# A hybrid diffusion backbone on one core: another queue for modulation weights, another order of the convolution's second product, and X formed half by half

## The chip, the cores and the metric

The kernel runs on one core of a Trainium2 chip. The time is the device time of the program in microseconds. Before the change three runs took 1233.27, 1236.50 and 1236.87 us, median 1236.5 us.

## The reference

Two layers run over 256 latent tokens of width 1024; 256 context tokens take part in layer 0. Each layer is a half-step FFN, a mixer and a half-step FFN, and each of these is

```python
h_lat = sublayer(h_lat, m_lat, 0, ffn1, FFN_HALF)
def sublayer(h, m, i, fn, res_w):
    y = fn(modulate(h, m[3 * i], m[3 * i + 1]))            # h * (1 + scale) + shift
    return layer_norm(ALPHA * h + res_w * m[3 * i + 2] * y, ln_g[l, i], ln_b[l, i])
def swiglu(h, w_in, w_out):
    gate, up = jnp.split(h @ w_in, 2, axis=-1)
    return (jax.nn.silu(gate) * up) @ w_out
```

The nine modulation vectors of a layer are `silu(c) @ w_ada[l] + b_ada[l]`, a product of one row with a 1024 x 9216 matrix. The mixer of layer 0 is differential attention with pooling. The mixer of layer 1 is a convolution module:

```python
a, g = jnp.split(h @ w_c1 + b_c1, 2, axis=-1)
z = a * jax.nn.sigmoid(g)
z = depthwise_conv(z, w_dw, 31 taps) + b_dw
z = jax.nn.silu(layer_norm(z, ln_g, ln_b))
return z @ w_c2 + b_c2
```

All inputs are float32.

## The kernel before

**Numbers.** A float32 product is made of three products of a reduced float32 format: each operand is split into a high part (a cast on ScalarE) and a low part (the difference, on VectorE), and `mm3` (L209) multiplies high by high, low by high and high by low. Activations are held as `XH` and `XL`, transposed: 128 channels on the partitions, eight channel blocks, tokens along the row.

**Weights.** All weights come as a list of jobs (`w_add`, L117), mostly 1 MB, in the order of use. `pump_load` (L120) issues a job's load on SP's queue into one of three `raw` buffers. Each job is cut into pieces of 1024 columns, here called weight tiles. `pump_split` (L143) makes the high part `wh` on ScalarE (L150) and the low part `wl` on VectorE (L151), or on GpSimd for a few of the convolution's; it takes buffers from the pool `wp` (six of each), or from another pool when the dictionary `alt` names one for that tile at the moment of the split. `wnext` (L154) hands out the next weight tile and splits up to five ahead.

**Order.** The program is traced in Python; a scheduler then orders the instructions of each engine by priority (the order of tracing, raised by `high_priority`) as they become ready in its own model of time. On the chip every engine works strictly in that order, and so does every queue of loads. `issue_after(i)` puts what is traced inside it behind instruction `i` on the same engine, without any other wait; `behind_x` (L277) does so behind the last forming of X.

**Modulation.** `ada_jobs` (L226) makes, for one modulation vector, eight pairs of a load (512 KB of weights, L236, on SP's queue) and a product with a sum on VectorE (L240), and a `fin` step on GpSimd (L248 to L257), which for a gate also writes the vector to DRAM and reads it back as a row over all partitions. The list `bg` holds them; `bgstep` (L289) is called once per weight tile in the FFNs and pops entries at an even rate (24, 32 and 8 products over 44 steps in the three lean FFNs), and `bg_one` (L265) issues the loads of the next entries before it pops one. In the lean FFNs (`sub_ffn`, L917) two load buffers rotate. They are the second FFN of layer 0, the first and the second of layer 1.

**The lean FFNs.** 44 weight tiles of the gate and up products, then 22 of the output product. The first two pairs of columns are done token tile by token tile: first 36 matmuls with token tile 0, then 36 with token tile 1, so that X of token tile 1 may be formed behind the first ones (`to_x_behind`). After them `flush` (L497) issues the affine part of the last layer norm of h on GpSimd (`affine`, L368): for each of two token tiles it loads the row `ln_g` on GpSimd's queue, multiplies two halves, loads `ln_b`, and adds two halves.

**X.** `to_x` (L321) transposes a normalized token tile on TensorE in two halves of four 128 x 128 blocks, scales and shifts each block (L333 on VectorE, L335 on ScalarE, in turn) and splits each half (L217): the high part on ScalarE, the low part on VectorE for the first half and on GpSimd for the second.

**The convolution module.** The first product takes 16 weight tiles. Four of the eight channel groups are convolved on TensorE with banded weights (L1137): for each group two runs (g) of 16 products into one PSUM tile, and after each run ScalarE takes it out (L1138). One group is done by ScalarE and GpSimd, three by VectorE, tap by tap (L998). `back` (L1041) transposes the finished groups, VectorE takes statistics, both engines normalize (`yn`), and TensorE transposes again before the SiLU (L1164) and the split. Six of the eight weight tiles of the second product are split ahead of the whole TensorE convolution (L1113). The second product (L1170 to L1184) computes the first 512 columns for both token tiles, then the other 512; `evac` (L383) adds the result to h, and `ln_norm` and `to_x` follow for each token tile.

## Time and profile before

| | |
|---|---|
| median of three runs | 1236.5 us |
| profiled execution | 1233.74 us |
| its span, first to last instruction | 1231.9 us |
| TensorE matmuls busy | 1181.1 us (96%) |
| VectorE busy | 882.7 us (72%) |
| ScalarE busy | 503.2 us (41%) |
| GpSimd busy | 206.7 us (17%) |
| mean granted clock of TensorE | 0.987 |
| loads from HBM | 269.38 MB, 220 GB/s over the span |

PE is TensorE, DVE is VectorE, ACT is ScalarE, POOL is GpSimd, SP is SyncE, which only issues loads. In a row of the timeline a bracket gives the idle time of that engine just before the row and what ended it; x is the number of instructions merged into the row. A matmul in full flow shows about 0.39 us, but they overlap: the distance of two starts is shorter. A granted clock of 1.00 is 2.4 GHz. In time, the second FFN of layer 0 lies at about 525 to 715 us, the first FFN of layer 1 at 715 to 921, the convolution module at 913 to 1037, and the last FFN behind it.

### The profile page before, as it was taken

What the parts mean: (1) busy time and instruction counts of PE and PEld (TensorE: products, weight loads), DVE (VectorE), ACT (ScalarE), POOL (GpSimd) and SP (SyncE); (2) the same over time, 40 slices, a digit from 0 to 9 for tenths busy, and PEclk for the clock granted to TensorE, in tenths of its full rate; (3) what the DMA queues carried; (4) which work ended last, traced back from release to release, by engine and by line L of the source; (5) the groups of instructions that cost most, each with busy time, mean ns of one, the idle gap of its engine ahead of it and who ended that gap; (6) DMA issues with size and microseconds to landing.
All of it is one profiled execution on the core that took longest, in us unless ns stands there. A gap on an engine that the chain in (4) does not pass through costs nothing.

```text
span 1231.9 us, 14930 instructions
## 1 busy us (share of the span) xinstructions
PE 1181.1 (96%) x5632; PEld 979.7 (80%) x5632; DVE 882.7 (72%) x1287; ACT 503.2 (41%) x731; POOL 206.7 (17%) x207
## 2 busy tenths in 40 slices
PE   6999999999999999999999999997999888999997
PEld 5888888888887887778888878886879877888885
DVE  5799987773337858798785688877667957875554
ACT  4243123222233546564444444433448333544431
POOL 0001020031003122134010033000017911330000
PEclk9899999999999999999999999998999989999999
DMA  9778688862232432369885748987648445975550
GB/s 361 306 252 290 230 275 308 271 223 100 86 124 65 161 137 103 137 233 336 329 299 186 265 167 337 326 315 274 220 164 297 145 178 168 322 279 184 175 188 35
DMA packets 59656, 272.60 MB, mean 221 GB/s; under 512 B 6592, under 2 KB 8256, under 8 KB 44224
## 3 DMA queue, kind: packets, MB, share of 16 engines
q1 hardware_dynamic: 56048, 259.56, 59.2%
q0 software_dynamic: 3536, 12.09, 3.0%
q8 instruction: 44, 0.72, 0.2%
q14 instruction: 28, 0.23, 0.1%
HBM read 269.38 MB, written 1.08 MB: 220 GB/s over the span
## 4 chain that ended last, share of the span: by engine, by line
PE 48%; DVE 7%; DMA 6%; ACT 2%; issue 2%; POOL 1%; DVEq 0%; SPq 0%; ACTq 0%; POOLq 0%
PE lf L212 7%; PE lf L210 6%; PE lf L211 6%; DMA ada<-in_wada 6%; PE of L210 4%; PE of L212 4%; PE of L211 4%; PE pc L1137 2%; DVE wl L151 2%; DVE ada L240 1%; PE c L210 1%; PE c L211 1%; PE c L212 1%; PE ltrf L435 1%; PE v L210 1%
## 5 line engine op out<-in xcount | busy, mean ns | idle before, releaser
L150 ACT CAST wh<-raw 128x1024 fp32r<-128x1024 f32 x309 | 321.6, 1051 | 466.6 <-PE of L212 128.3
L151 DVE TENSOR_TENSOR wl<-raw,wh 128x1024 fp32r<-128x1024 f32 x302 | 379.2, 1271 | 150.3 <-ACT wh L150 149.3
L210 PE MATMUL lf<-wh,XH 128*128 128x512 f32 x528 | 208.5, 395 | 3.8 <-ACT XH L217 3.6
L240 DVE SCALAR_TENSOR_TENSOR ada<-ada,crow 128x1024 f32<-128x1024 f32 x128 | 163.1, 1282 | 68.3 <-DMA ada<-in_wada 67.6
L212 PE MATMUL lf<-wh,XL 128*128 128x512 f32 x528 | 207.0, 392 | 0.4 <-DVE XL L217 0.4
L211 PE MATMUL lf<-wl,XH 128*128 128x512 f32 x528 | 206.0, 390 | 0.0
L210 PE MATMUL of<-wh,GHf 128*128 128x512 f32 x344 | 135.1, 393 | 0.0
L212 PE MATMUL of<-wh,GLf 128*128 128x512 f32 x344 | 134.5, 391 | 0.0
L211 PE MATMUL of<-wl,GHf 128*128 128x512 f32 x344 | 134.5, 391 | 0.0
L210 PEld LDWEIGHTS lf<-wh,XH 128*128 128x128 f32 x528 | 99.2, 188 | 25.0 <-ACT XH L217 5.5
L212 PEld LDWEIGHTS lf<-wh,XL 128*128 128x128 f32 x528 | 99.1, 188 | 23.2 <-DVE XL L217 2.3
L211 PEld LDWEIGHTS lf<-wl,XH 128*128 128x128 f32 x528 | 99.2, 188 | 20.0
L211 PEld LDWEIGHTS of<-wl,GHf 128*128 128x128 f32 x344 | 65.0, 189 | 13.4
L212 PEld LDWEIGHTS of<-wh,GLf 128*128 128x128 f32 x344 | 64.9, 189 | 13.6
L210 PEld LDWEIGHTS of<-wh,GHf 128*128 128x128 f32 x344 | 65.0, 189 | 13.3
L248 POOL TENSOR_TENSOR m<-m,cols 128x8 f32<-128x8 f32 x19 | 13.9, 731 | 358.0 <-DVE ada L240 213.3
L210 PE MATMUL gf<-XH,wh 128*128 128x512 f32 x152 | 59.1, 389 | 0.0
L211 PE MATMUL gf<-XL,wh 128*128 128x512 f32 x152 | 59.1, 389 | 0.0
L212 PE MATMUL gf<-XH,wl 128*128 128x512 f32 x152 | 59.1, 389 | 0.0
L210 PE MATMUL uf<-XH,wh 128*128 128x512 f32 x152 | 59.1, 389 | 0.0
L211 PE MATMUL uf<-XL,wh 128*128 128x512 f32 x152 | 59.1, 389 | 0.0
L212 PE MATMUL uf<-XH,wl 128*128 128x512 f32 x152 | 59.1, 389 | 0.0
(296 smaller groups left out, 1948.2 us busy)
## 6 DMA issues: line engine op xcount, KB each, us to landing
raw<-in_wfl SPq DMA_DIRECT2D x66, 1024.0 KB, 6.8
ada<-in_wada SPq DMA_DIRECT2D x128, 512.0 KB, 5.4
raw<-in_wfo SPq DMA_DIRECT2D x40, 1024.0 KB, 5.0
raw<-in_wfi SPq DMA_DIRECT2D x22, 1024.0 KB, 6.2
raw<-in_wc SPq DMA_DIRECT2D x10, 1024.0 KB, 6.6
wcv<-in_wcv SPq DMA_DIRECT2D x16, 512.0 KB, 4.7
aw<-in_wsh SPq DMA_DIRECT2D x8, 512.0 KB, 10.4
aw<-in_wsc SPq DMA_DIRECT2D x8, 512.0 KB, 9.9
```

The lines of the kernel that those rows point to most:

```text
L150: act.copy(wh[:, :w], r[:, off:off + w])
L151: lo_ins[q] = (pool if q in pool_lo else dve).tensor_tensor(wl[:, :w], r[:, off:off + w], wh[:, :w].bitcast(F32), ALU.subtract)
L210: pe.matmul(ps, lh, rh, start=first, stop=False)
L211: pe.matmul(ps, lh, rl, start=False, stop=False)
L212: last_mm[0] = pe.matmul(ps, ll, rh, start=False, stop=last)
L240: dve.scalar_tensor_tensor(st["raw"] if s == streams[-1] else crow["junk"], st["raw"], 1.0, crow[s], ALU.mult, ALU.mult, accum_out=mcol[l, ...
L248: pool.tensor_tensor(m, m, col("bad", (l * 9 + v) * 8, 8), ALU.add)
L435: pe.transpose(tr[:, j * W + t * P:j * W + (t + 1) * P], sg[:, t, j * P:(j + 1) * P], ident)
L1137: last = pe.matmul(pc[:, g * P:(g + 1) * P], wt[:, tap % 8 * P:(tap % 8 + 1) * P], z2, start=tap == 0, stop=tap == 15)
```

## The change

The second product's weights are loaded by depth quarter, both column halves in one load. The modulation loads of the lean FFNs go to GpSimd's queue; the first two of them are issued after X of token tile 1, ahead of the affine steps; each product on VectorE is placed behind the newest weight split. In `to_x` the scalings of the second half are placed behind the first half's, and on ScalarE behind the first half's cast. Six splits that were traced ahead of the TensorE convolution are traced two by two behind the evacuations of its first three runs. The second product does all of token tile 0, then all of token tile 1; the splits of the following weight tiles and the evacuations are placed by hand.

```diff
--- before.py
+++ after.py
@@ -195,9 +195,8 @@
         w_add(a["wcl"][:, hh * 2048:(hh + 1) * 2048], (1024, 1024))
     for j in range(2, 8):
         w_add(a["wc1"][j].rearrange("u p f -> p u f"), (1024, 1024))
-    for n in range(2):
-        for kk in range(2):
-            w_add(a["wc2"][n, :, kk * 2048:(kk + 1) * 2048], (1024, 1024))
+    for q in range(4):
+        w_add(a["wc2"][:, :, q * 1024:(q + 1) * 1024].rearrange("n p f -> p n f"), (1024, 1024))
     add_ffn(1, 1, 2, PARTS2)
     for ji, (_, widths) in enumerate(jobs):
         off = 0
@@ -222,6 +221,7 @@
     bg = []
     cur_ada = [None]
     NADS = [3]
+    ada_queue = [nc.sync]
 
     def ada_jobs(l, v, streams, gate=None, then=None):
 
@@ -233,7 +233,7 @@
 
             def load(j=j, st=st):
                 st["raw"] = cur_ada[0].tile([P, D], F32, tag="adaraw", name=f"ada{l}{v}{j}", bufs=NADS[0])
-                nc.sync.dma_start(st["raw"], a["wada"][l, v, j])
+                ada_queue[0].dma_start(st["raw"], a["wada"][l, v, j])
 
             def unit(j=j, st=st):
                 for s in streams:
@@ -262,12 +262,18 @@
 
     rate = [0.0, 0.0]
 
-    def bg_one():
+    def bg_load():
         for pre, _, _ in bg[:NADS[0]]:
             if pre is not None and id(pre) not in done:
                 done[id(pre)] = pre
                 pre()
-        with behind_x():
+
+    def bg_one():
+        bg_load()
+        with behind_x(), ExitStack() as st:
+            if ada_queue[0] is pool:
+
+                st.enter_context(tc.issue_after(lo_ins[len(ready) - 1].ins))
             bg.pop(0)[1]()
 
 
@@ -322,6 +328,7 @@
 
         xm = xmp[0].tile([P, KT, P], F32, tag="xm", bufs=xmp[1], name="xm" + name)
         ins = []
+        xd = xa = None
         for half in range(2):
             tr = trt(f"tr{name}{half}")
             for j in range(4):
@@ -329,12 +336,17 @@
                 pe.transpose(tr[:, j * P:(j + 1) * P], src_of[:, k * P:(k + 1) * P], ident)
             for j in range(4):
                 k = half * 4 + j
-                if func == AF.Identity and j % 2 == 0:
-                    dve.tensor_scalar(xm[:, k, :], tr[:, j * P:(j + 1) * P], A[:, k:k + 1], B[:, k:k + 1], ALU.mult, ALU.add)
-                else:
-                    act.activation(xm[:, k, :], tr[:, j * P:(j + 1) * P], func, bias=B[:, k:k + 1], scale=A[:, k:k + 1])
+                with ExitStack() as after:
+                    for i in (xd, xa):
+                        if i is not None:
+                            after.enter_context(tc.issue_after(i.ins))
+                    if func == AF.Identity and j % 2 == 0:
+                        xd = dve.tensor_scalar(xm[:, k, :], tr[:, j * P:(j + 1) * P], A[:, k:k + 1], B[:, k:k + 1], ALU.mult, ALU.add)
+                    else:
+                        xa = act.activation(xm[:, k, :], tr[:, j * P:(j + 1) * P], func, bias=B[:, k:k + 1], scale=A[:, k:k + 1])
             sl = slice(half * 4, half * 4 + 4)
             ins.append(split(XH[:, sl, tok0:tok0 + P], XL[:, sl, tok0:tok0 + P], xm[:, sl, :], pool if half else dve))
+            xa = ins[-1][0]
         last_pow[0] = ins[1][1]
         if tok0 < SEQ:
             anchors[:] = ins[0][1], ins[1][0]
@@ -494,6 +506,8 @@
                                 turn_last()
                                 turns.append((sg[f], q + f - ff, f))
                     if ff == 0:
+                        with tc.issue_after(last_pow[0].ins):
+                            bg_load()
                         flush()
             final = p1 == NFF
             for n in range(2):
@@ -918,6 +932,7 @@
         with ExitStack() as st:
             cur_ada[0] = st.enter_context(tc.tile_pool(name=f"ada{l}{i}", bufs=1, side="right"))
             NADS[0] = 2
+            ada_queue[0] = pool
             for (gl, gv, f) in gates:
                 ada_jobs(gl, gv, (0,), gate=f)
             for ml, mi, mln in mods:
@@ -1109,8 +1124,6 @@
             for t in range(2):
                 pool.tensor_tensor(h[t], h[t], lnr[0], ALU.mult)
                 pool.tensor_tensor(h[t], h[t], lnr[1], ALU.add)
-        with tc.issue_after(warm_ins.ins):
-            pump_split(q0 + 22)
         tapstep(len(taps))
         def back_after(ins, *js):
             with tc.issue_after(ins.ins):
@@ -1135,7 +1148,10 @@
                         if tap == 0 and last is not None:
                             after.enter_context(tc.issue_after(last.ins))
                         last = pe.matmul(pc[:, g * P:(g + 1) * P], wt[:, tap % 8 * P:(tap % 8 + 1) * P], z2, start=tap == 0, stop=tap == 15)
-                act.activation(cvp[j][:, g, :], pc[:, g * P:(g + 1) * P], AF.Identity, bias=col("bd2", 2 * j + g))
+                got = act.activation(cvp[j][:, g, :], pc[:, g * P:(g + 1) * P], AF.Identity, bias=col("bd2", 2 * j + g))
+
+                with tc.issue_after(got.ins):
+                    pump_split(q0 + 16 + min(6, 2 * (2 * n + g + 1)))
                 if (j, g) in BACK:
                     back_after(last, *BACK[j, g])
         with tc.high_priority(HP):
@@ -1152,7 +1168,7 @@
             mr = c2.tile([P, 2], F32, name="cmr", bufs=1)
             dve.scalar_tensor_tensor(mr, mv[:, :, 0], -1.0, rs, ALU.mult, ALU.mult)
             for t in range(2):
-                dve.tensor_scalar(yn[t][:, 0:512], cvt[t, 0], mv[:, t, 0:1], rs[:, t:t + 1], ALU.subtract, ALU.mult)
+                yn_ins = dve.tensor_scalar(yn[t][:, 0:512], cvt[t, 0], mv[:, t, 0:1], rs[:, t:t + 1], ALU.subtract, ALU.mult)
                 act.activation(yn[t][:, 512:1024], cvt[t, 1], AF.Identity, bias=mr[:, t:t + 1], scale=rs[:, t:t + 1])
             for j0 in range(0, 8, 2):
                 tr = trt(f"ytr{j0}")
@@ -1166,18 +1182,37 @@
                                    AF.Silu, bias=col("cvb", j), scale=col("cvg", j))
                 sl = slice(j0, j0 + 2)
                 split(XH[:, sl, SEQ:2 * SEQ], XL[:, sl, SEQ:2 * SEQ], cv[:, sl, :])
-        spare(c2, taken[0] + 4, 3, None, bufs=3)
-        for n in range(2):
-            pss = [mmt(f"c2{n}{t}") for t in range(2)]
-            with tc.issue_after(silu.ins), tc.issue_after(wcv_ins[0].ins):
-                ws = [wnext(AHEAD + (n == 1 and j == 3)) for j in range(4)]
-            for t, k in [(t, 2 * q + kk) for q in range(4) for t in range(2) for kk in range(2)] if n == 0 else \
-                    [(t, k) for t in range(2) for k in range(KT)]:
-                out_mm(pss[t], t, XH, XL, SEQ, k, k % 2, ws[k // 2], k == 0, k == KT - 1)
-                if k < KT - 1:
+
+        spare(c2, taken[0], 6, None, bufs=3)
+        for q in (0, 2, 4):
+            del alt[taken[0] + q]
+        for q in (6, 7):
+            alt[taken[0] + q] = lambda name: c2.tile([P, 1024], F32R, tag="wcv", name=name, bufs=5)
+        with tc.issue_after(got.ins), tc.issue_after(wcv_ins[0].ins), tc.issue_after(yn_ins.ins):
+            pump_split(q0 + 24)
+        with tc.high_priority(HP), tc.issue_after(silu.ins):
+            pump_split(q0 + 27)
+        pump_load(qmap[q0 + 29][0] + 1)
+        pss = {(t, n): mmt(f"c2{n}{t}") for t in range(2) for n in range(2)}
+        ws = {}
+        for t in range(2):
+            for n, q in [(n, q) for q in range(4) for n in range(2)] if t == 0 else [(n, q) for n in range(2) for q in range(4)]:
+                if t == 0:
+                    ws[n, q] = wnext(8 - len(ws))
+                elif (n, q) in ((0, 1), (0, 2)):
+                    with tc.issue_after(norm_ins[0].ins):
+                        pump_split(q0 + 27 + q)
+                for k in (2 * q, 2 * q + 1):
+                    with ExitStack() as after:
+                        if t and (n, k) == (0, 0):
+                            after.enter_context(tc.issue_after(last_mm[0].ins))
+                        out_mm(pss[t, n], t, XH, XL, SEQ, k, k % 2, ws[n, q], k == 0, k == KT - 1)
+                if q < 3:
                     continue
-                with tc.high_priority(HP):
-                    evac(pss[t], t, n, G, True, ALPHA, f"c2{n}{t}", f"d{t}")
+                with tc.high_priority(HP), tc.issue_after(lo_ins[q0 + 26].ins), ExitStack() as after:
+                    if t:
+                        after.enter_context(behind_x())
+                    evac(pss[t, n], t, n, G, True, ALPHA, f"c2{n}{t}", f"d{t}")
                     if n == 1:
                         ln_norm(t, f"d{t}")
                         A, B = AB[1, 2, 0]
```

## Rows read from the trace of the kernel before

**Rows 1.** The page, busy time of each engine.
```profile
PE 1181.1 (96%) x5632; PEld 979.7 (80%) x5632; DVE 882.7 (72%) x1287; ACT 503.2 (41%) x731; POOL 206.7 (17%) x207
```

**Rows 2.** Windows: stretch, length; busy us (instructions) of each engine; TensorE's clock, DMA share, GB/s.
```profile
840.00:860.00 20.00, 13.40 (x54) 10.40 (x54) 16.15 (x22) 6.30 (x10) 2.88 (x5) 0.83 0.78 280
860.00:880.00 20.00, 20.00 (x90) 16.56 (x89) 10.23 (x10) 8.98 (x9) 0.00 (x0) 1.00 0.65 217
...
960.00:980.00 20.00, 15.66 (x124) 15.46 (x122) 19.86 (x33) 8.26 (x11) 18.59 (x20) 0.91 0.38 116
```

**Rows 3.** Timeline of TensorE, first FFN of layer 1: start, duration, what [idle before <-releaser].
```profile
715.02 0.50 PE L210 MATMUL lf<-wh,XH 128*128 128x512 f32 x1
...
852.91 0.69 PE L435 MATMUL ltrf<-ident,lsgf 128*128 128x128 f32 x2 [5.42 <-DVE lsgf L470]
...
913.09 0.50 PE L210 MATMUL cl<-wh,XH 128*128 128x512 f32 x1
```

**Rows 4.** Timeline of TensorE, the convolution (a product has two records).
```profile
963.15 3.84 PE L1137 MATMUL pc<-zd,wcv 128*128 128x128 f32 x32
971.33 8.93 PE L1137 MATMUL pc<-zd,wcv 128*128 128x128 f32 x64 [4.34 <-ACT cv L1138]
980.72 3.95 PE L1137 MATMUL pc<-zd,wcv 128*128 128x128 f32 x32 [0.46 <-ACT cv L1138]
```

**Rows 5.** Timeline of ScalarE, the convolution.
```profile
965.25 5.76 ACT L150 CAST wh<-raw 128x1024 fp32r<-128x1024 f32 x6
970.92 0.36 ACT L1138 ACTIVATE cv<-pc,cols 128x128 f32<-128x128 f32 x1
```

**Rows 6.** Timeline of TensorE, end of the second product and start of the FFN.
```profile
1032.37 1.08 PE L329 MATMUL trd<-ident,h 128*128 128x128 f32 x8 [0.52 <-DVE h L315]
...
1037.06 0.50 PE L210 MATMUL lf<-wh,XH 128*128 128x512 f32 x1 [2.45 <-ACT XH L217]
```

**Rows 7.** Timeline of VectorE, the last tap of channel group 2.
```profile
983.96 0.47 DVE L998 SCALAR_TENSOR_TENSOR cv<-zp,wd,acc 128x256 f32<-128x256 f32 x1
```

**Rows 8.** Timeline of ScalarE, the second product.
```profile
1016.59 1.06 ACT L150 CAST wh<-raw 128x1024 fp32r<-128x1024 f32 x1 [0.91 <-PE c L212]
```

**Rows 9.** Timeline of VectorE, end of that first FFN, and the second product.
```profile
907.30 0.69 DVE L301 BATCH_NORM_STATS2 bstf<-h 128x6 f32<-128x512 f32 x1
...
1020.39 1.23 DVE L151 TENSOR_TENSOR wl<-raw,wh 128x1024 fp32r<-128x1024 f32 x1 [1.50 <-ACT wh L150]
1021.54 1.28 DVE L386 TENSOR_TENSOR evc<-c,grow 128x512 f32<-128x512 f32 x2
...
1023.94 1.28 DVE L301 BATCH_NORM_STATS2 bstd<-h 128x6 f32<-128x512 f32 x2
```

**Rows 10.** Timeline of ScalarE, X of token tile 0 before the convolution.
```profile
910.99 1.40 ACT L335 ACTIVATE xm<-tr,mB,mA 128x128 f32<-128x128 f32 x3 [9.52 <-DVE xm L333]
```

**Rows 11.** Waits of SP's queue, 715 to 855: in total, times, longest.
```profile
SPq L236 <- DVE lsgf L470: 40.8, 10, 9.2
SPq L129 <- DVE wl L151: 38.4, 21, 6.1
```

**Rows 12.** Timeline of VectorE, first and last of 32 modulation products, layer 1's first FFN.
```profile
724.78 1.22 DVE L240 SCALAR_TENSOR_TENSOR ada<-ada,crow 128x1024 f32<-128x1024 f32 x1
...
853.16 1.23 DVE L240 SCALAR_TENSOR_TENSOR ada<-ada,crow 128x1024 f32<-128x1024 f32 x1 [0.31 <-DMA ada<-in_wada]
```

**Rows 13.** Timeline of GpSimd, first and last affine step in that FFN.
```profile
727.09 0.65 POOL L372 DMA_DIRECT2D ln_g<-in_ln_g  x1
...
764.84 2.53 POOL L375 TENSOR_TENSOR h<-h,ln_b 128x512 f32<-128x512 f32 x2 [6.51 <-DMA ln_b<-in_ln_b]
```

**Rows 14.** Loads issued 765 to 855: size, median us from issue to landing.
```profile
ada<-in_wada SPq DMA_DIRECT2D x21, 512.0 KB, 5.7
```

**Rows 15.** Loads issued 715 to 770 on GpSimd's queue.
```profile
ln_g<-in_ln_g POOLq DMA_DIRECT2D x2, 512.0 KB, 5.8
ln_b<-in_ln_b POOLq DMA_DIRECT2D x2, 512.0 KB, 7.1
```

## The prediction

> **What bounds the kernel now.** I read the page's busy times first: TensorE's matmuls fill 96% of the span, and no other engine passes 80% [rows 1]. So only stretches in which TensorE stops, or runs at its lower clock, can give time back, and the windows show where they are [rows 2]. The profiled execution was 1233.74 us, 1.8 us around its span of 1231.9 us; it stands 2.8 us below the median of the runs, 1236.5 us. I work out differences in the profile and take them off the median.
>
> Three places touch the change. (a) At the end of the gate and up products of layer 1's first FFN TensorE stood still for 5.42 us, waiting for VectorE [rows 3]; the stretch 840 to 860 has 54 matmuls where the next has 90 at 20.00/90 = 0.222 us each [rows 2], so 36 x 0.222 = 8.0 us are lost there, clock included. (b) In the convolution TensorE did its first group of 16 products in 3.84 us, stood 4.34 us, and needed 8.93 us for the next two, where 2 x 3.84 = 7.68 would do [rows 4]. ScalarE was busy with six weight casts, 5.76 us in a row, and took the first result out only at 970.92 [rows 5]. (c) After the second product TensorE stopped 0.52 us before the transposes and 2.45 us after them, until X of token tile 0 was there [rows 6].
>
> **The change, part by part.**
>
> *Casts behind the convolution's evacuations.* The six splits come now two at a time behind each of the first three evacuations. The evacuation of the first group then meets a free ScalarE; the row at 980.72 shows what remains when it does, 0.46 us. Gain 4.34 - 0.46 = 3.9, and with the clock that sank after the stop (0.91 in this stretch [rows 2]) 8.93 - 7.68 = 1.25 more: 5.1 us. Each step has 3.84 us on TensorE, and ScalarE needs 0.36 + 2 x 0.96 = 2.3 us, so it keeps up. What is late next: the transposes of channel groups 0 and 2, which would now come at 979.5, need the tap sum that VectorE ended at 984.43 [rows 7]. The six splits that VectorE ran among the taps now stand behind them in the program, so the sum should end near 976; if it doesn't, up to 5 us are given back. Bounds 0 to 5.5; I take 5.1.
>
> *The second product by token tile.* 96 matmuls before and after. Token tile 0 is finished 48 matmuls, 10.7 us, before the end instead of 24, which would cover the 3.0 us of (c). But all eight weight tiles must now stay until token tile 1 has used them. The first six were split before the line that gives three of them other buffers (the alternatives are looked up when a tile is split), so they fill all six buffers of the weight pool. The next three casts wait for token tile 1 to use up the first of them, as the casts wait on TensorE now [rows 8], and the change orders token tile 0's evacuation on VectorE behind the third of these splits. With T the end of token tile 0: three tiles are used up at T + 3 x 6 x 0.222 = T + 4.0; 0.3, a cast of 1.06 [rows 8] and a split of 1.23 [rows 9] bring T + 6.6. Six evacuation steps take 1021.54 to 1025.22 [rows 9], 3.7, to T + 10.3. From the end of such statistics to the first product took 907.99 to 913.09, 5.1 us, at the end of that first FFN [rows 9, 3]; with the next edit's 0.47 off it is 4.6, so T + 14.9. Token tile 1 ends at T + 10.7 and the eight transposes take 1.1 [rows 6], so TensorE loses T + 14.9 - (T + 11.8) = 3.1 us, what it loses now, and I add 0.5 for token tile 1, whose evacuation stands behind X of tile 0. Taken: +0.5. Bounds: -3 if those casts find buffers, +4 if the third must wait for a tile of the other column half.
>
> *X half by half.* ScalarE does three of its four scalings, 1.40 us, before it casts the first half [rows 10]; the third now comes after the cast. 1.40/3 = 0.47 us earlier at each place where TensorE waits for that half. I count three places outside (c) at which it truly stands: 1.5 us. Bounds 0 and 3. VectorE's two later scalings were in time already.
>
> *Modulation weights on GpSimd's queue, and their products behind the split.* 64 loads of the three lean FFNs leave SP's queue; all loads go on to the same buffers, two of them. What it removes is waiting in order: in the first FFN of layer 1 SP stood 38.4 us for weight loads' buffers and 40.8 us for modulation loads', each with the other kind behind it [rows 11]. What it adds: (i) each product on VectorE comes behind the newest split, so the first, now at 724.78 [rows 12], cannot come before tile 12 is split. Its buffer is free after 84 matmuls (18.7) and 1.1 of transposes behind 715.02 [rows 3], and 0.3 + 1.06 + 1.23 later: 737.4. (ii) The loads stand on GpSimd behind the affine steps, in which GpSimd waits for its own rows from 727.09 to 767.4, four times about 10 us [rows 13]. The first two loads are issued before them; the third can be issued only after the first product, behind whatever rows were queued first. Queued behind it in turn: the next loads, and on VectorE every split that follows that product; TensorE waits for those.
>
> The price in the first FFN of layer 1: 32 loads went in 724.78 to 854.4, 4.05 us each [rows 12], which is 8.1 for each of the two buffers: landing 5.7 [rows 14], product 1.2, the rest 1.2 of queueing. The program gives 32 products to 44 tiles, so a split follows every 0.727 x 4.05 = 2.95 us where TensorE needs 12 x 0.222 and a share of transposes, 2.75. Over 44 tiles the splits lose 44 x 0.2 = 9 us; they start five tiles less 2.6 us ahead, 11 us. By itself that just closes without a stop. The affine steps take from this lead: behind two of the four blocks, now quicker since nothing else loads (8 to 9 us each), the third load goes out at about 746 instead of 739, and when the blocks end, near 763, I put the lag at 9 us. Stop: 9 + 9 - 11 = 7 us, against 8.0 now: a gain of 1.0. The ends: no lag and the same landing, no stop, a gain of 8; third load behind three blocks (lag 16) and landing as ln_b's rows on GpSimd's queue, 7.1 [rows 15], so 0.73 x (8.1 + 1.4)/2 = 3.47 a tile, 44 x 0.72 = 32, a stop of 37, or 29 more than now. ln_g's row, 5.8 [rows 15], is the nearer, since it is what the same queue needs with little beside it; lag 16 alone gives 14, 6 more. I keep -8 to +15. In the other two FFNs the pace is one product in 5 and in 15 us, and the lead of 11 us covers a lag of 9; at lag 16 the earlier one stops 3 us.
>
> The Trainium skill, DMA: Bandwidth & Descriptors, section Issuing engines are not separate DMA queues, says that transfers started from several engines share the same DMA engines, and that another issuer saves only the issuing time. By it this part is worth 0 and the sum below would be 1 us smaller. The trace agrees as far as the DMA engines go, 0.78 busy in 840 to 860 [rows 2], but shows in the same FFN the 38.4 and 40.8 us of in-order waiting that the rule leaves out.
>
> The same weights in another cut, for the second product, keep 1 MB a load, and a later weight load has its buffer in time: 0.
>
> Sum: -5.1 + 0.5 - 1.5 - 1.0 = -7.1; profiled execution 1233.74 - 7.1 = 1226.6, and from the median 1229.4. I say 1229.
>
> **Rivals.** *The stream is freed* (15%): weight loads no longer stand behind modulation loads, the lag stays under the lead. For it: SP's waits; against it: 4.05 us a load is mostly landing and product, which stay. The stop goes: 1229.4 - 7 = 1222, with the buffers of (c) found as well 1219. *GpSimd's order starves VectorE* (20%): the third to sixth loads stand behind three or four blocks of the affine steps, VectorE waits in order at the third product and the splits behind it run out. It decides from a lag of some 13 us in the first FFN of layer 1, since lead and pace leave 2 and the present stop is 8, and the convolution's 6 must be lost as well. With lag 16 and landing 0.5 longer: 44 x 0.38 = 17 + 16 - 11 = 22, 14 more than now, and 3 in the FFN before it: 1236.5 - 6.1 + 17 = 1247; half of it 1240. For it: 40 us of affine steps with four row waits [rows 13]; against it: two loads are ahead of them and the pace is slow at first. *The convolution gains and the rest gives it back* (20%): evacuation behind the third split 4 us later, the stop in the FFN 2 to 4 us longer: 1229.4 + 7 = 1236, no change.
>
> **How the numbers follow.** Forecast 45%: 1224 to 1232. 0.3% is 3.7 us, about what a measurement here can tell. Faster by more: 45 + 15 = 60%; within: 20%; slower: 20%. Leaving out some of the freed case's best end and the starved case's far end gives 1219 to 1243.
>
> **What would show it.** Right: between the first and second group of the convolution TensorE stops about half a microsecond and ScalarE's casts stand two by two; the tap sum of groups 2 ends before 980; three casts of the next FFN wait for TensorE during token tile 1, with a stop of about 3 us before that FFN; the half's cast comes behind two scalings; the first modulation product of layer 1's first FFN near 737, and a stop of several microseconds in its last third. Wrong: no stop there, or a stop already at 750 to 770; no stop between second product and FFN.

## The result and the profile after

The changed kernel takes 1256.05 us (median of four runs, 1248.8 to 1260.44) against 1234.89 for the kernel before: ratio 1.0172, 95% interval 1.0148 to 1.0196. It is slower by 1.7%, and the forecast of 1229 us (1219 to 1243) was wrong in sign. The profiled execution took 1260.44 us with a span of 1258.7; it is the longest of the four, so the differences of the profiles, 26.8 us in all, stand 5.6 us above the difference of the medians.

The first reading is by stages: in each timeline of TensorE, the start of the first product of a stage.

| stage, us | before | after | difference |
|---|---|---|---|
| all up to the second FFN of layer 0 | 525.7 | 526.7 | +0.9 |
| second FFN of layer 0 | 189.3 | 189.4 | +0.2 |
| first FFN of layer 1 | 198.1 | 218.5 | +20.4 |
| convolution's first product | 50.1 | 50.2 | +0.2 |
| TensorE's convolution, to the transposes of its norm | 42.3 | 38.5 | -3.8 |
| from there to the last FFN (second product) | 31.6 | 34.1 | +2.5 |
| last FFN, to TensorE's last matmul | 186.6 | 189.0 | +2.3 |
| from there to the end of the span | 8.2 | 12.3 | +4.0 |

One stage holds three quarters of what the profiles differ by. The page of the changed kernel (busy us, share and instructions of each engine; a group of instructions with its busy time, mean ns, and the idle time before it; loads with their queue, number and median landing), against [rows 1] and [rows 14], with the products' line of the page before under it:

```profile
PE 1191.1 (95%) x5632; PEld 984.4 (78%) x5632; DVE 875.2 (70%) x1287; ACT 501.9 (40%) x731; POOL 236.1 (19%) x271
...
L240 DVE SCALAR_TENSOR_TENSOR ada<-ada,crow 128x1024 f32<-128x1024 f32 x128 | 160.1, 1258 | 96.4 <-DMA ada<-in_wada 95.3
...
ada<-in_wada SPq DMA_DIRECT2D x64, 512.0 KB, 4.9
ada<-in_wada POOLq DMA_DIRECT2D x64, 512.0 KB, 5.6
```

```profile
L240 DVE SCALAR_TENSOR_TENSOR ada<-ada,crow 128x1024 f32<-128x1024 f32 x128 | 163.1, 1282 | 68.3 <-DMA ada<-in_wada 67.6
```

A load is no slower on GpSimd's queue (5.6 us; 5.7 before in the busy stretch), yet VectorE waits 95.3 us for modulation loads over the whole program, 67.6 before; in the first FFN of layer 1 it is 46.1 against 24.4. The loads start late. GpSimd's timeline in the first FFN of layer 1 shows why:

```profile
729.47 1.18 POOL L236 DMA_DIRECT2D ada<-in_wada  x2
730.64 0.53 POOL L384 DMA_DIRECT2D ln_g<-in_ln_g  x1
738.36 2.54 POOL L387 TENSOR_TENSOR h<-h,ln_g 128x512 f32<-128x512 f32 x2 [7.19 <-DMA ln_g<-in_ln_g]
...
755.62 2.53 POOL L387 TENSOR_TENSOR h<-h,ln_g 128x512 f32<-128x512 f32 x2 [4.47 <-DMA ln_g<-in_ln_g]
758.10 0.59 POOL L236 DMA_DIRECT2D ada<-in_wada  x1
...
788.89 0.60 POOL L255 DMA_DIRECT2D gd<-m  x1 [0.29 <-POOL m L252]
796.08 0.54 POOL L257 DMA_DIRECT2D grow<-gd  x1 [6.59 <-DMA gd<-m]
796.61 1.15 POOL L236 DMA_DIRECT2D ada<-in_wada  x2
```

Two loads go out, then three blocks of the affine steps, each with a wait for its own row, then the third load at 758.10. VectorE's first and third product and the last, against [rows 12]:

```profile
744.53 1.22 DVE L240 SCALAR_TENSOR_TENSOR ada<-ada,crow 128x1024 f32<-128x1024 f32 x1
...
762.09 1.23 DVE L240 SCALAR_TENSOR_TENSOR ada<-ada,crow 128x1024 f32<-128x1024 f32 x1 [9.26 <-DMA ada<-in_wada]
...
894.92 0.09 DVE L240 DVE_READ_ACCUMULATOR ada<-ada,crow 128x1 f32 x1
```

Before the product at 762.09 VectorE stands for 9.26 us, with the weight splits behind it in order. TensorE's timeline, against [rows 3], shows splits missing 13 us later and a stop of 6.08 us at the FFN's end, where the kernel before (second block) had 0.60:

```profile
716.10 0.50 PE L209 MATMUL lf<-wh,XH 128*128 128x512 f32 x1
...
775.42 0.50 PE L210 MATMUL lf<-wl,XH 128*128 128x512 f32 x1 [2.83 <-DVE wl L151]
...
930.06 1.94 PE L336 MATMUL tr<-ident,h 128*128 128x128 f32 x8 [6.08 <-DVE h L321]
...
934.60 0.39 PE L209 MATMUL cl<-wh,XH 128*128 128x512 f32 x1
```

```profile
909.81 1.08 PE L329 MATMUL tr<-ident,h 128*128 128x128 f32 x8 [0.60 <-DVE h L315]
```

That last stop comes from late splits too: token tile 0's evacuation, at 926.11 on VectorE, stands behind six splits of the convolution's weights, and these behind loads that found their buffers late:

```profile
917.14 2.00 ACT L150 CAST wh<-raw 128x1024 fp32r<-128x1024 f32 x2 [2.99 <-DMA raw<-in_wcl]
```

```profile
918.23 4.84 DVE L151 TENSOR_TENSOR wl<-raw,wh 128x1024 fp32r<-128x1024 f32 x4 [2.82 <-ACT wh L150]
923.84 2.36 DVE L151 TENSOR_TENSOR wl<-raw,wh 128x1024 fp32r<-128x1024 f32 x2 [0.76 <-ACT wh L150]
926.11 0.68 DVE L398 TENSOR_TENSOR evf<-of,grow 128x512 f32<-128x512 f32 x1
```

Stops over 0.25 us add up to 20.9 us in this FFN, against 7.8 before. The other 7 of the 20.4 us are in the main the lower clock that follows such stops: TensorE's granted clock was 0.50 for 17.1 us of this FFN, 6.8 before. In the windows it is the third number from the right, 0.83 to 0.91 where full speed is 1.00:

```profile
760.00:780.00 20.00, 16.76 (x70) 13.09 (x69) 13.51 (x18) 5.23 (x7) 5.33 (x6) 0.91 0.75 271
...
860.00:880.00 20.00, 18.15 (x76) 14.47 (x75) 15.41 (x21) 7.28 (x9) 2.31 (x5) 0.91 0.71 241
920.00:940.00 20.00, 13.38 (x57) 10.43 (x56) 14.16 (x24) 6.60 (x10) 2.70 (x5) 0.83 0.52 186
```

In the convolution the change did what it says. ScalarE takes each run out at once and casts two tiles behind it, where [rows 5] had six casts in a row, and TensorE stops 0.46 us where [rows 4] had 4.34:

```profile
988.71 0.37 ACT L1151 ACTIVATE cv<-pc,cols 128x128 f32<-128x128 f32 x1 [1.69 <-PE pc L1150]
988.98 1.98 ACT L150 CAST wh<-raw 128x1024 fp32r<-128x1024 f32 x2
```

```profile
989.13 7.04 PE L1150 MATMUL pc<-zd,wcv 128*128 128x128 f32 x59 [0.46 <-ACT cv L1151]
...
1017.52 0.51 PE L1068 MATMUL cvt<-ident,cv 128*128 128x128 f32 x2 [1.13 <-DVE cv L1013]
```

The new 1.13 us come from VectorE: the six splits now fall among the taps later, three of them beside GpSimd's 1024-wide steps, where they take 2.72, 3.01 and 3.01 us; the other three take 1.21:

```profile
1002.48 3.01 DVE L151 TENSOR_TENSOR wl<-raw,wh 128x1024 fp32r<-128x1024 f32 x1
...
1009.13 1.21 DVE L151 TENSOR_TENSOR wl<-raw,wh 128x1024 fp32r<-128x1024 f32 x1
```

```profile
1001.05 6.68 POOL L1126 TENSOR_TENSOR h<-h,clnr 128x1024 f32<-128x1024 f32 x2
```

At the end of the second product, ScalarE, VectorE and TensorE in this order, against [rows 6, 8, 9]:

```profile
1042.66 1.05 ACT L150 CAST wh<-raw 128x1024 fp32r<-128x1024 f32 x1 [10.85 <-PE c L211]
```

```profile
1043.75 3.95 DVE L151 TENSOR_TENSOR wl<-raw,wh 128x1024 fp32r<-128x1024 f32 x3 [11.21 <-ACT wh L150]
1047.61 1.28 DVE L398 TENSOR_TENSOR evc<-c,grow 128x512 f32<-128x512 f32 x2
```

```profile
1053.07 1.08 PE L336 MATMUL trd<-ident,h 128*128 128x128 f32 x8 [0.81 <-DVE h L321]
1057.48 0.79 PE L209 MATMUL lf<-wh,XH 128*128 128x512 f32 x1 [3.33 <-ACT XH L216]
1058.07 0.63 PE L210 MATMUL lf<-wl,XH 128*128 128x512 f32 x1
```

VectorE was free for 11.21 us, and token tile 0's evacuation stood behind three splits whose casts waited for buffers that TensorE still read. TensorE then ran dry, and the first twelve products of the FFN came 0.43 us apart instead of 0.23, at a granted clock of 0.66 over 1055 to 1065.

### The profile page after: what moved, and what is told of

It reads as the page before. It is cut to its first block, busy times and chain, and to the rows that moved or that the text cites. A ratio compares the mean times of both kernels' runs of the same rounds, so it can differ in the third digit from the quotient of the medians.

```text
span 1258.7 us, 14934 instructions
## 1 busy us (share of the span) xinstructions
PE 1191.1 (95%) x5632; PEld 984.4 (78%) x5632; DVE 875.2 (70%) x1287; ACT 501.9 (40%) x731; POOL 236.1 (19%) x271
## 3 DMA queue, kind: packets, MB, share of 16 engines
q0 software_dynamic: 12752, 45.65, 10.7%
## 5 line engine op out<-in xcount | busy, mean ns | idle before, releaser
L240 DVE SCALAR_TENSOR_TENSOR ada<-ada,crow 128x1024 f32<-128x1024 f32 x128 | 160.1, 1258 | 96.4 <-DMA ada<-in_wada 95.3
L211 PE MATMUL lf<-wh,XL 128*128 128x512 f32 x528 | 209.7, 397 | 0.6 <-POOL XL L216 0.4
L236 POOL DMA_DIRECT2D ada<-in_wada x64 | 34.6, 541 | 198.4 <-DVE ada L240 198.2
```

What stands on the lines that cost most here:

```text
L211: last_mm[0] = pe.matmul(ps, ll, rh, start=False, stop=last)
L236: ada_queue[0].dma_start(st["raw"], a["wada"][l, v, j])
L240: dve.scalar_tensor_tensor(st["raw"] if s == streams[-1] else crow["junk"], st["raw"], 1.0, crow[s], ALU.mult, ALU.mult, accum_out=mcol[l, ...
```

## The experiments

Ratios are to the kernel before, run on the same chip beside each.

**The loads back on SyncE's queue** (from the changed kernel)
```
-            ada_queue[0] = pool
```


> The changed kernel with the modulation loads back on SyncE's queue (and so without the edge on the products, which hangs on the queue); the other two parts stay. Theory A, GpSimd's order starves VectorE in the first FFN of layer 1: that FFN, 218.5 us in the changed kernel against 198.1 before, comes back to 197 to 200, and the time to 1231 to 1237. Rival B, the new second product and the half-by-half X cost the time (the last FFN's late clock, the later splits): the FFN stays above 212 and the time above 1248.

Measured: 1237.22 us, ratio 1.0023 (1.0003 to 1.0043). The FFN takes 195.6 us, and the end comes 8.3 us behind the last matmul. Theory A holds: the queue, with the edge that hangs on it, costs 1.0172 - 1.0023, 1.5% or some 18 us. But the rest is no gain either.

**The queue part alone** (from the kernel before)
```
+            if ada_queue[0] is pool:
+                st.enter_context(tc.issue_after(lo_ins[len(ready) - 1].ins))
...
+                        with tc.issue_after(last_pow[0].ins):
+                            bg_load()
...
+            ada_queue[0] = pool
```


> The kernel before with the modulation loads on GpSimd's queue and the edge on their products alone. Theory A: the first FFN of layer 1 goes from 198.1 to 213 to 220 us, with a first stop of TensorE at 765 to 780 and one of over 4 us at the FFN's end; the time is 1249 to 1258. Rival B: the FFN stays under 203 and the time under 1241, since the queue costs only beside the other parts.

Measured: 1250.32 us, ratio 1.0123 (1.0090 to 1.0156). The FFN takes 208.8, with a first stop of 2.97 us, up to 764.59, and one of 6.11 at its end. The time is theory A's; the FFN is 4 us below its range, though far above rival B's. So this FFN loses 10.7 us by the queue alone, and 20.4 in the changed kernel. The third load is as late here (756.61), but from the third product to the last they come 4.08 us apart, in the changed kernel 4.43. Why is open: of the other two parts only X half by half touches this FFN, and no run has the queue with that part alone.

**The affine steps left out of that FFN** (from the changed kernel)
```
-                    if ln != (1, 0):
+                    if ln != (1, 0) and (l, i) != (0, 1):
```


> The changed kernel without the affine steps (four row loads, eight multiplies and adds on GpSimd) at the start of the first FFN of layer 1; they are left out of the computation. Theory A1, the affine steps hold the third to fifth load up: the third load is issued before 750 instead of 758.1, the stops up to 810 go (about 6 us) and much of what follows, and the FFN falls from 218.5 to 203 to 210. Theory A2, the wait for the gate's row on the same queue (6.6 and 5.9 us) is what counts: the FFN stays at 214 or above.

Measured: 1242.33 us, ratio 1.0064 (1.0043 to 1.0086); the FFN 199.8. The third load goes out at 748.07, and not GpSimd's work but VectorE's product holds it:

```profile
748.07 0.53 POOL L236 DMA_DIRECT2D ada<-in_wada  x1 [14.40 <-DVE ada L240]
```

No stop over 0.5 us comes before 851, one of 4.74 us stays at the end. Theory A1 holds, with an FFN 3 us shorter than it said: 1.0172 - 1.0064 is 13 of the 18 us. The stop at the end is not the affine steps' doing, since it stays without them; with the loads on SyncE's queue it is gone. The FFN before this one took 193.7 us here instead of 189.4, which wasn't looked into. The run leaves the affine steps' own work out too; since the kernel with the loads on SyncE's queue keeps that work and its FFN takes 195.6, the work alone isn't the price, the order is.

**The gate's two transfers on SyncE's queue** (from the changed kernel)
```
-                pool.dma_start(dr, m)
+                nc.sync.dma_start(dr, m)
...
-                pool.dma_start(mrow[l, v, s], ...)
+                nc.sync.dma_start(mrow[l, v, s], ...)
```


> The changed kernel with the gate's two small transfers (column to memory, memory to row) on SyncE's queue in place of GpSimd's; the modulation loads stay on GpSimd's. Theory A2: the 6.6 and 5.9 us in which no load is issued go, and the FFN falls from 218.5 to 205 to 211. Theory A1: the FFN stays at 214 or above. If SyncE's queue then waits for the column in its turn, raw weights come later and the FFN gets longer than 218.5.

Measured: 1254.46 us, ratio 1.0169 (1.0131 to 1.0207); the FFN 218.3. Theory A2's FFN did not come. But the two waits did not go either, they changed queues: in this FFN SyncE's queue stood 13.0 us for the column's transfer (two waits, the longer 9.4), with the raw weights behind it. So moving them gains nothing, and what the two holes of 6 us cost by themselves isn't shown.

**The edge without the queue, and the queue without the edge** (from the kernel before)
```
+            if edge[0]:
+                st.enter_context(tc.issue_after(lo_ins[len(ready) - 1].ins))
...
+                        with tc.issue_after(last_pow[0].ins):
+                            bg_load()
...
+            edge[0] = True
```


> The kernel before with the modulation loads still on SyncE's queue and only the edge added that holds each product of the modulation behind the newest weight split (with the first two loads asked for at the FFN's start). Theory E, the edge makes VectorE wait: the first FFN of layer 1 takes 203 us or more against 198.1. Theory A, GpSimd's queue does: it stays at 195 to 200 and the time within 1231 to 1237 against 1233.

Measured: 1240.72 us, ratio 1.0048 (1.0032 to 1.0065); the FFN 204.6. Theory E's FFN, and a time above theory A's: the edge alone costs 0.5%. VectorE takes the first product at 739.74, before at 724.78, and TensorE stops for splits already in the first half:

```profile
771.01 0.80 PE L211 MATMUL lf<-wl,XH 128*128 128x512 f32 x1 [2.80 <-DVE wl L151]
```

The other half of the pair (from the kernel with the queue part alone):
```
-                st.enter_context(tc.issue_after(lo_ins[len(ready) - 1].ins))
```


> The kernel before with the modulation loads on GpSimd's queue, without the edge on their products. Theory A: the FFN is as long as with both (208.8 in the profile of the queue part alone) to 4 us, the time 1244 to 1256, the chip's end 11 to 12.5 us behind TensorE's last matmul as with both. Theory E: the FFN is at 203 or below and the time under 1242.

Measured: 1288.64 us, ratio 1.0430 (1.0394 to 1.0467), far above what theory A said. The second FFN of layer 0, 189 to 194 us in all other versions, takes 211.6, the first of layer 1 217.4. Its first large stop:

```profile
581.39 0.80 PE L211 MATMUL lf<-wl,XH 128*128 128x512 f32 x1 [4.46 <-DVE wl L151]
```

So neither theory is the whole: the edge costs 0.5% on SyncE's queue and saves 3% on GpSimd's, where a product that stands ahead of a split makes the split wait for the late load too: here VectorE stood 4.94 us for a load before the product at 578.36, and the split that TensorE waited for came at 580.12.

**The casts behind the evacuations alone** (from the kernel before)
```
-        with tc.issue_after(warm_ins.ins):
-            pump_split(q0 + 22)
...
+                with tc.issue_after(got.ins):
+                    pump_split(q0 + 16 + min(6, 2 * (2 * n + g + 1)))
```


> The kernel before with one edit alone: the last six splits of the second product's weights are no longer asked for before TensorE's convolution but two at a time behind its evacuations. Theory C: TensorE's convolution with its evacuations, 42.3 us before, takes 38.5 as in the changed kernel, nothing after it is late (31.6 us from there to the last FFN, which takes 186.6), and the time is 1228 to 1232 against 1234. Rival D, the casts moved come late to the second product: the 3.8 us come back there as a longer second product (34 us and more) and the time stays within 1233 to 1236.

Measured: 1228.84 us, ratio 0.9964 (0.9950 to 0.9977). The convolution takes 38.5 us, the stage behind it 31.9, the FFN 186.6. Theory C holds; nothing is given back.

**The second product by token tile alone** (from the kernel before)
```
+            w_add(a["wc2"][:, :, q * 1024:(q + 1) * 1024]..., (1024, 1024))
...
+                with tc.high_priority(HP), tc.issue_after(lo_ins[q0 + 26].ins), ...:
```


> The kernel before with the convolution's second product by token tile alone (the new layout of its weights, the order of its matmuls and the edges on its evacuations). Theory C: the second product's stage goes from 31.6 to 33 to 34 us and the last FFN from 186.6 to 189, its first matmuls at the low granted clock; the time is 1236 to 1240. Rival D: the stage's growth in the changed kernel came from the casts moved, and here it stays at 31.6 and the FFN at 186.6, time 1232 to 1236.

Measured: 1237.56 us, ratio 1.0027 (1.0012 to 1.0042); the stage 34.2, the last FFN 188.3, with the stop and the slow products of the changed kernel. Theory C holds.

**X half by half alone** (from the kernel before)
```
+                    for i in (xd, xa):
+                        if i is not None:
+                            after.enter_context(tc.issue_after(i.ins))
```


> The kernel before with X formed half by half on VectorE and ScalarE alone. If it does what was forecast, 1.0 to 1.5 us go over all FFN starts and the time is 1232 to 1233.5 against 1234; if the order that it sets costs as much as it gives, the time is 1233.5 to 1236 and the start of the first FFN of layer 1 stays 190 us behind that of the FFN before it.

Measured: 1238.44 us, ratio 1.0030 (1.0012 to 1.0047), worse than either expectation. X of token tile 0 of the first FFN of layer 1, first in the kernel before, then here:

```profile
712.41 1.80 DVE L333 TENSOR_SCALAR xm<-tr,mA,mB 128x128 f32<-128x128 f32 x4 [0.36 <-PE tr L329]
...
716.06 1.29 POOL L217 TENSOR_TENSOR XL<-xm,XH 128x512 fp32r<-128x512 f32 x1 [5.04 <-ACT XH L217]
```

```profile
713.90 0.41 DVE L338 TENSOR_SCALAR xm<-tr,mA,mB 128x128 f32<-128x128 f32 x1 [0.36 <-PE tr L330]
714.40 0.46 ACT L340 ACTIVATE xm<-tr,mB,mA 128x128 f32<-128x128 f32 x1 [8.84 <-DVE xm L338]
714.89 0.73 DVE L338 TENSOR_SCALAR xm<-tr,mA,mB 128x128 f32<-128x128 f32 x2 [0.59 <-ACT xm L340]
...
717.09 0.68 DVE L392 TENSOR_TENSOR evf<-of,grow 128x512 f32<-128x512 f32 x1
717.70 0.40 DVE L338 TENSOR_SCALAR xm<-tr,mA,mB 128x128 f32<-128x128 f32 x1
...
719.32 1.28 POOL L217 TENSOR_TENSOR XL<-xm,XH 128x512 fp32r<-128x512 f32 x1 [6.82 <-ACT XH L217]
...
720.66 0.50 PE L212 MATMUL lf<-wh,XL 128*128 128x512 f32 x1 [0.42 <-POOL XL L217]
```

Before, VectorE did its four scalings in a row. Here the second waits 0.59 us for ScalarE's first, and the fourth, at 717.70, comes behind ScalarE's third, the first half's low part and the other token tile's evacuation. The first half is no earlier (its cast starts 1.93 us behind the first scaling, before 1.94), and GpSimd's low part starts 719.32 - 713.90 = 5.42 us behind the first scaling instead of 716.06 - 712.41 = 3.65. TensorE now waits for it, 0.4 to 0.7 us at five places in the second FFN of layer 0, the first of layer 1 and the convolution's first product, and the second FFN of layer 0 takes 190.3 us instead of 189.3.

**Casts and X half by half together** (both diffs above)

> The kernel before with the casts behind the evacuations and X half by half; the queue and the second product as before. By theory C the sum of the two alone: 1227 to 1232 against 1234. By rival D within 1232 to 1236.

Measured: 1234.15 us, ratio 1.0007 (0.9993 to 1.0021). Rival D's number, but for another reason: the two run alone, -0.36 and +0.30%, add up to it within the interval. With +0.27% for the second product the sum is +0.21%, and the changed kernel without its queue part measured +0.23%.

**The second product by token tile, without the edge behind the split** (from the kernel before; the second with the casts too)
```
-                with tc.high_priority(HP), tc.issue_after(lo_ins[q0 + 26].ins), ExitStack() as after:
+                with tc.high_priority(HP), ExitStack() as after:
```


> The kernel before with the second product by token tile alone, and without the edge that holds the evacuations of a token tile behind the first split of the last FFN's weights. Theory F, this edge gives the gain away: in the changed kernel VectorE stands idle for 11.2 us with token tile 0's evacuation queued behind that split. Then the stage from the convolution's norm to the last FFN takes 27 to 30 us, against 34.2 with the edge and 31.6 before, the first matmuls of the FFN run at the high granted clock, and the time is 1226 to 1231 against 1233. Rival G, the order of the matmuls itself costs it: the stage stays above 33 and the time above 1235.

> As e11, with the casts behind the evacuations too. By theory F the two gains add up: 38.5 us for TensorE's convolution, 27 to 30 for the stage behind it, and 1221 to 1227 against 1233. By rival G 1231 to 1235.

Measured: 1232.31 us, ratio 0.9983 (0.9968 to 0.9999), and 1227.24 us, ratio 0.9950 (0.9933 to 0.9966). Theory F holds, with stages of 29.2 and 29.7 us and times a little above its own: one edge turned +0.27% into -0.17%. VectorE and TensorE of the second kernel:

```profile
1014.84 0.69 DVE L385 TENSOR_TENSOR evc<-c,grow 128x512 f32<-128x512 f32 x1 [6.79 <-PE c L211]
```

```profile
1023.79 1.08 PE L328 MATMUL trd<-ident,h 128*128 128x128 f32 x8 [0.47 <-DVE h L314]
...
1028.41 0.40 PE L211 MATMUL c<-wh,XL 128*128 128x512 f32 x1
1028.65 0.39 PE L209 MATMUL lf<-wh,XH 128*128 128x512 f32 x1
```

The evacuation waits for its product alone, token tile 1's matmuls fill the time until X is there, and the FFN follows the last of them without a stop, at a granted clock of 1.00. This second kernel is 0.5% faster than the kernel before, and faster than the changed one.

**X half by half, each engine behind its own steps alone** (from the kernel with X half by half alone, and on the best kernel)
```
+                    i = xd if on_dve else xa
```


> X half by half on the kernel before, with each engine's steps ordered behind its own steps alone, so that VectorE and ScalarE no longer take turns. Theory H, the turns cost it: GpSimd's split of the second half begins 3.3 to 4 us behind the first step on X, as in the kernel before (3.65), against 5.4 with the turns; the stops of TensorE behind that split go, and the time is 1230 to 1234 against 1233. Theory I, the order by halves costs it: the time stays at 1236 to 1239.

> The casts behind the evacuations, the second product by token tile without the edge behind the weight split, and X half by half with own edges. By theory H 1224 to 1228 against 1233, no slower than without X half by half (ratio 0.995); by theory I 1229 to 1233.

Measured: 1239.44 us, ratio 1.0062 (1.0045 to 1.0079), and 1231.73 us, ratio 0.9997 (0.9982 to 1.0013). Theory H falls. The same turns stand in the trace, with GpSimd's low part as late (5.43 us), so the order by halves sets them: in it scalings of one transposed half wait for each other across the engines. The times of the kernel before fit the order half 0, half 1, half 0, half 1, though its rows don't name the halves; what makes the engines wait wasn't looked for. The FFN's 201.7 us, 3 more than with the other edges, weren't looked into. On the best kernel X half by half takes 0.5% away.

**The queue part without the last FFN** (from the kernel with the queue part alone)
```
+            ada_queue[0] = nc.sync if (l, i) == (1, 1) else pool
```


> The kernel before with the queue part alone, but the last FFN's modulation loads on SyncE's queue again. If the late end comes from the last FFN's loads on GpSimd's queue, the end is 8.2 to 8.4 us behind TensorE's last matmul instead of 12.2 and the time 1244 to 1248, against 1250 with the queue in all three FFNs. If it is set earlier, the end stays 11 to 12.3 us behind and the time at 1248 to 1252.

Measured: 1249.71 us, ratio 1.0145 (1.0126 to 1.0165), the end 11.6 us behind the last matmul. The late end doesn't come from the last FFN's loads.

## Why the prediction was wrong

**The step that failed** is the price of the modulation loads on GpSimd's queue: a gain of 1.0 us forecast, a loss of 15 (alone) to 18 us (in the whole) measured. In the first FFN of layer 1, for which it was worked out, the profiles show 10.7 and 20.4 us lost. The mechanism was there; its sizes were too small, and one place had no term.

- *The lag.* The first product was put at 737.4 and came at 744.53. The third load was put at 746, 7 us behind the end of the first product and behind two blocks of affine steps; it went out at 758.10, behind three, 12 us behind the end of the first product at 745.7. The lag taken was 9.
- *The pace.* 4.05 us a load was 4.43 from the third product to the last (762.09 to 895.0 for 30).
- With these the prediction's own formula gives 44 x (0.727 x 4.43 - 2.75) + 12 - 11 = 22 us of stop instead of 7. The traces agree: the 601st of this FFN's 792 products starts 11.9 us later than before, on top of the 8.0 lost there before. With the queue alone, lag 13 and pace 4.08 give 11 to 12, and the 601st product is 3.4 us later. So the lag by itself is worth 2 to 3 us, and the slower pace of the changed kernel most of the rest. That pace hangs on the affine steps too, since without them it is 4.12; why they slow it in the whole and not in the queue part alone is open.
- *No term at all* stood for the FFN's end. The stop before the last transposes with the slow products behind it is 6.7 of the 20.4 us, and 7.0 of the 10.7 with the queue alone.

So the rival "GpSimd's order starves VectorE" is what happened. Its sign, a stop already at 750 to 770, came at 772.6, and at 761.6 with the queue alone. Its price, 14 us in this FFN, was 20; its 3 us in the FFN before did not come (+0.2). The range ended at 1243, below this rival's own 1247. The lag of 13 us from which it was to decide doesn't follow from the formula either: at the forecast's pace 9 + 16 - 11 - 8 = 6, so it takes 16 to lose the convolution's gain.

The Trainium skill, DMA: Bandwidth & Descriptors, section Issuing engines are not separate DMA queues, puts another issuer at the issuing time it saves. The landings agree with that, 5.6 and 5.7 us; the time does not, since by it this part was worth 0. What decided was the order of the issuing engine's other work, as the run without the affine steps shows.

**Casts behind the evacuations**: right. 5.1 forecast, 3.8 in the profile, 4.4 by the ratio; what is missing in the profile is in the main the 1.13 us behind the slow splits. The tap sum that was to end near 976 ended at 999.15, which is 977.5 when the start of TensorE's convolution is set to that of the kernel before.

**The second product**: mechanism right almost to the row. The third split was put 6.6 us behind token tile 0's end and the FFN 14.9; that product ended near 1041, the splits at 1047.7, the FFN began at 1057.48. The term was +0.5 and measured +0.27%, 3.3 us, inside its bounds: in the profile 1.2 us more of stop, and the FFN's slow first products, which no term held. The prediction knew the edge and priced it; what it didn't see is that without the edge the part is a gain.

**X half by half**: wrong in sign, -1.5 forecast, +3.7 measured by the ratio. The step that failed is "VectorE's two later scalings were in time already": the fourth became late, and with it GpSimd's low part.

**Not in the forecast at all**: the 4 us at the end of the program.

## What to carry to other kernels

Before you move loads to the queue of an engine that also computes, list everything that engine waits for between two of them: the loads inherit each wait, and so does every engine that consumes them in order. When you move a wait off a queue, look for it on the queue that you move it to. An edge that orders urgent work behind unrelated work is worth a run without it, and an order that takes turns between two engines on the same data must be priced on both.

## What was not expected of the hardware

All six kernels with modulation loads on GpSimd's queue end 11.1 to 12.3 us behind TensorE's last matmul, and all eleven others 8.2 to 8.3. SyncE's last wait, before and after:

```profile
SPq L1288 <- PEq L1288: 0.7, 2, 0.5
```

```profile
SPq L1323 <- PEq L1323: 4.6, 2, 4.1
```

The profile puts it down to TensorE's queue. Its cause stays open.

A split on VectorE took 3.01 us beside GpSimd's 1024-wide additions and 1.21 us without. The Trainium skill, SBUF — State Buffer, section Terms, calls the pair of ports that the two engines share exclusive for a whole instruction; the rows agree: 3.01 - 1.21 = 1.8 us more, less than the 3.3 of one of those additions. No run here took GpSimd's steps away to show it.
